# Emptying the merges' PSUM results by one engine each, and moving the output's scaled part, in a gated delta-rule block

## The chip, the cores and the metric

The kernel runs on one core of one Trainium2 chip. The metric is device time in microseconds of one execution. The kernel before was run three times: median 951.15 us, lowest 949.65, highest 952.15.

## The reference

One residual block with 512 tokens of width 1024, batch 1, all in float32. Two token mixers run on the normalised input: a gated delta rule with 8 heads of width 128, and a convolution branch with a causal depthwise convolution over 31 frames. Their gated sum goes through an output projection; a SwiGLU channel mixer with 2816 hidden units and a last RMSNorm follow. The part that matters here is the delta rule, cut to its core:

```python
kk = jnp.einsum("bnhid,bnhjd->bnhij", k, k)
m_low = jnp.where(strict, beta[..., :, None] * kk * decay, 0.0)
t_mat = m_low + jnp.eye(CHUNK)
sol = lax.linalg.triangular_solve(t_mat, rhs, left_side=True, lower=True, unit_diagonal=True)
u, w = sol[..., :DV], sol[..., DV:]
...
def step(S, xs_c):
    v_new = u_c - w_c @ S
    o_c = qd_c @ S + a_c @ v_new
    S = S * el_c + k_dec_c.T @ v_new
    return S, o_c
```

For each head a unit lower triangular system is solved per chunk, and a state S of 128x128 runs over the chunks.

## The kernel before, in words

**Stages.** The first stage makes all projections of the normalised input (query, key, value and output gate of each head, the two halves of the convolution branch, the branch gates) and, woven into them, the delta rule and the 31-tap convolutions. The attention output projection, the convolution branch's projection, the output projection and the channel mixer follow. The change lies in the first stage alone, from about 100 to 435 us of the span.

**Projections.** Float32 weights are split into a high and a low part: `unit` loads a 128x1024 piece, ScalarE rounds it (`whi`, L111) and VectorE subtracts (`wlo`, L112). A product is three matmuls with 512 columns each (`split3`, L121). `proj` yields after each of the eight row blocks, so one step of the driver is three such matmuls. There are three buffers for weight pieces, so ScalarE's next L111 often waits for TensorE to finish with an older piece.

**The order of the work.** The loop at the end of the stage (`while step() or chains`) takes one projection step at a time. `count` is the number of steps done. The delta rule of a head is a Python generator (`chain`); each `yield n` puts its next piece n steps later, so that a product of the chain stands n projection steps behind the operations that make its operands. The chain of head h begins 32 + `OTHERS[h]` steps after the one before. The framework turns the traced order into a fixed order on each engine when the kernel is built: by priority, which is the order of tracing, among what it thinks ready, with all waits added by it. `behind()` puts a piece of the chain behind the last marked projection operation of each engine. The 31-tap convolutions (`conv31`) are traced with a priority lowered by `OFF`, so they fill VectorE where it has nothing else ready: 30 operations of 512 columns a channel block (L690), accumulating in one PSUM bank. After the eighth block the sum over blocks (`sacc`, L696) is the operand of L709, the first product of the layer norm, which stands in TensorE's order among the products of the attention output projection.

**The chain of a head.** The kernel uses chunks of 128 tokens, four per head, and inverts the triangular matrices by doubling: GpSimd makes the inverses of 16-wide diagonal blocks (L499 to L504), and three merges make 32, 64 and 128-wide inverses. A merge is two products after one another, each for two pairs of chunks (`group`, L526), into one PSUM tile (`psb`, a pool with a single buffer, tile name `b`), and each result is emptied to SBUF, partly transposed in 32x32 blocks:

- The 16-wide merge ends in L574 and L575 on VectorE.
- The 32-wide merge's first product is emptied by L587. Its second is emptied by six operations, L595 to L600, in turn on ScalarE (copies) and VectorE (transposes). L595 and L596 write `m64`, the operand of the next merge; L597 to L600 write `Y`, the inverse that is being built. L601 copies one corner of `Y`.
- The 64-wide merge's first product is emptied by L605 (ScalarE) and L606 (VectorE), its second by L609 (ScalarE) and L610 (VectorE).

Then the recurrence runs over n = 0 to 3 with one PSUM tile a step (`pst`, a single buffer of one bank, tile name `st`, four column blocks of 128): L622 and L623 multiply the state by key and query (blocks 0 and 2), L625 on VectorE makes the right-hand side R, L628 applies `Y` to it (block 1), and L630 on ScalarE scales the result to the solution `w`. Three steps later L633 makes the state's update (block 0) and L634 the output's inner part (block 3). VectorE makes the new state (L640, or L638 for n = 0); ScalarE scales block 2 by the decay (`Ae`, L646), VectorE adds block 3 to it (L647; for n = 0, L643 copies block 3 alone) and ScalarE takes the sum of squares (L648). Three steps later the next n begins. L646 and L647 exist for n = 1, 2 and 3, 24 times in all.

The framework keeps the accesses of different engines to one PSUM tile apart, reads among them: L596 starts when L595 has ended, though they read other partitions.

Of the kernel before, what the change touches and what calls it, by code (L numbers as in the profile page):

```python
# [6 lines left out]
F32 = mybir.dt.float32  # L7
F32R = mybir.dt.float32r
I32 = mybir.dt.int32
AF = mybir.ActivationFunctionType  # L10
# [4 lines left out]
P = 128  # L15
# [17 lines left out]
def block_kernel(ctx, tc, a):  # L33
    nc = tc.nc
    V, S, G, PE = nc.vector, nc.scalar, nc.gpsimd, nc.tensor
# [176 lines left out]
    with tc.tile_pool(name="st", bufs=2) as st:  # L212
# [78 lines left out]
        ps = psg.tile([P, 4, P], F32, name="g")  # L291
# [61 lines left out]
        beta, nbeta, kdf, egc, negc, egl, nmc = (sm[:, i] for i in range(7))  # L353
# [28 lines left out]
    gp = ph1.enter_context(tc.tile_pool(name="gp", bufs=1))  # L382
    gps_.append(gp)
    Ys = [gp.tile([P, NT, P], F32, name="Y%d" % i) for i in range(2)]
    st16, st32, st64 = ([gp.tile([P, 2, P], F32, name="s%d%d" % (w, i)) for i in range(2)] for w in (16, 32, 64))
    m64 = gp.tile([P, 2, 64], F32, name="m64")
# [3 lines left out]
    def even_odd(t):  # L390
        return t.rearrange("p (q e) c -> p e q c", e=2)
# [137 lines left out]
    def chain(h, kT, qT, ss, kd, b2, Un, cp, Vp, at, yq, zs):  # L529
        sq, Y = junk[:, 0:P], Ys[h % 2]  # L530
        flat = lambda t: t.rearrange("p n c -> p (n c)")
        b32 = [slice(32 * b, 32 * b + 32) for b in range(4)]
        lo64, hi64 = slice(0, 64), slice(64, P)
        ev, od = slice(0, 2), slice(2, 4)
        Ue, Uo = (even_odd(Un)[:, e] for e in range(2))


        cT = gp.tile([P, 2, 32], F32, name="cT")
        V.transpose(out=flat(cT), in_=flat(cp[:, od]))
        s1 = gp.tile([P, 2, 32], F32, name="s1")  # L540
        S.activation(s1[:, :, 0:16], cT[:, :, 0:16], AF.Copy, scale=mh2)
        S.activation(s1[:, :, 16:32], cp[:, ev, 16:32], AF.Copy, scale=mh1)
        for b in b32:
            S.copy(out=st16[0][b, :, b], in_=s1[b])
        yield 3
        for i in (0, 2):
            S.copy(out=st32[0][b32[i], :, b32[i + 1]], in_=Ue[b32[i], :, b32[i + 1]])
            V.transpose(out=st32[0][b32[i + 1], :, b32[i]], in_=Uo[b32[i], :, b32[i + 1]])
        yield 3
        S.copy(out=st64[0][lo64, :, hi64], in_=Ue[lo64, :, hi64])  # L550
        S.copy(out=st64[0][hi64, :, lo64], in_=Uo[lo64, :, hi64])
        yield 3


        YY = gp.tile([P, NT, 32], F32, name="YY")
        XX = gp.tile([P, NT, 32], F32, name="XX")
        S.activation(YY[:, :, 0:16], yq, AF.Copy, scale=mh1)
        S.activation(YY[:, :, 16:32], yq, AF.Copy, scale=mh2)
        V.transpose(out=flat(XX), in_=flat(YY))
        Xe, Xo, Ye, Yo = XX[:, ev], XX[:, od], YY[:, ev], YY[:, od]  # L560
        m = gp.tile([P, 2, 16], F32, name="m16")
        V.tensor_tensor(out=m, in0=Xe[:, :, 0:16], in1=Yo[:, :, 16:32], op=ALU.add)
        s2 = gp.tile([P, 2, 32], F32, name="s2")
        S.copy(out=s2[:, :, 16:32], in_=Ye[:, :, 16:32])
        S.copy(out=s2[:, :, 0:16], in_=Xo[:, :, 0:16])
        for b in b32:
            S.copy(out=st16[1][b, :, b], in_=s2[b])
        yield 3
        ps = group(16, st16[0], m)
        Q = gp.tile([P, 2, 16], F32, name="Q16")  # L570
        S.activation(Q, ps, AF.Copy)
        yield 3
        ps = group(16, st16[1], Q)
        V.scalar_tensor_tensor(out=Xe[:, :, 0:16], in0=ps, scalar=mh2, in1=Xe[:, :, 0:16], op0=ALU.mult, op1=ALU.add)  # L574
        V.scalar_tensor_tensor(out=Yo[:, :, 16:32], in0=ps, scalar=mh1, in1=Yo[:, :, 16:32], op0=ALU.mult,  # L575
                               op1=ALU.add)
        m = gp.tile([P, 2, 32], F32, name="m32")
        for i, b in enumerate(b32):
            (S.copy if i < 2 else V.tensor_copy)(out=m[b], in_=Yo[b] if i % 2 else Xe[b])
        V.transpose(out=flat(Xo), in_=flat(Yo))  # L580
        V.transpose(out=flat(Ye), in_=flat(Xe))
        for i, b in enumerate(b32):
            S.copy(out=st32[1][b, :, b], in_=Ye[b] if i % 2 else Xo[b])  # L583
        yield 4
        ps = group(32, st32[0], m)
        Q = gp.tile([P, 2, 32], F32, name="Q32")
        S.activation(Q, ps, AF.Copy)  # L587
        for i in range(2):
            S.copy(out=m64[b32[i], :, b32[i]], in_=Xe[b32[i]])
            S.copy(out=m64[b32[i + 2], :, b32[i]], in_=Xo[b32[i]])  # L590
        for b in b32:
            S.copy(out=Y[b, :, b], in_=YY[b])  # L592
        yield 4
        ps = group(32, st32[1], Q)
        S.copy(out=m64[b32[1], :, b32[0]], in_=ps[b32[1]])  # L595
        V.transpose(out=m64[b32[3], :, b32[0]], in_=ps[b32[0]])  # L596
        S.copy(out=Y[b32[2], od, b32[3]], in_=ps[b32[2]])  # L597
        V.transpose(out=Y[b32[2], ev, b32[3]], in_=ps[b32[3]])
        S.copy(out=Y[b32[0], od, b32[1]], in_=ps[b32[0]])
        V.transpose(out=Y[b32[0], ev, b32[1]], in_=ps[b32[1]])  # L600
        S.copy(out=Y[lo64, ev, hi64], in_=Y[hi64, od, hi64])  # L601
        yield 5

        ps = group(64, st64[0], m64)
        S.activation(st64[1][hi64, :, hi64], ps[hi64], AF.Copy)  # L605
        V.tensor_copy(out=st64[1][lo64, :, lo64], in_=ps[lo64])  # L606
        yield 4
        ps = group(64, st64[1], Y[:, ev, hi64])
        S.activation(Y[lo64, ev, hi64], ps[hi64], AF.Copy)  # L609
        V.tensor_copy(out=Y[lo64, od, hi64], in_=ps[lo64])  # L610
        yield 3


        o = gp.tile([P, NT, P], F32, name="o", bufs=3)
        Sp = None
        for n in range(NT):

            ps = pst.tile([P, 4, P], F32, name="st")
            if n == 0:
                R = Vp[:, 0, :]  # L620
            else:
                PE.matmul(ps[:, 0, :], kT[:, n, :], Sp, start=True, stop=True)  # L622
                PE.matmul(ps[:, 2, :], qT[:, n, :], Sp, start=True, stop=True)  # L623
                R = gp.tile([P, P], F32, name="R", bufs=3)
                V.scalar_tensor_tensor(out=R, in0=ps[:, 0, :], scalar=negc[:, n, h:h + 1], in1=Vp[:, n, :],  # L625
                                       op0=ALU.mult, op1=ALU.add)
                yield 3
            PE.matmul(ps[:, 1, :], Y[:, n % 2 * 2 + n // 2, :], R, start=True, stop=True)  # L628
            w = gp.tile([P, P], F32, name="w", bufs=2)
            S.activation(w, ps[:, 1, :], AF.Copy, scale=b2[:, n:n + 1])  # L630
            yield 3
            if n < NT - 1:
                PE.matmul(ps[:, 0, :], kd[:, n, :], w, start=True, stop=True)  # L633
            PE.matmul(ps[:, 3, :], at[:, n, :], w, start=True, stop=True)  # L634
            if n < NT - 1:
                Sn = gp.tile([P, P], F32, name="S", bufs=2)
                if n == 0:
                    V.tensor_copy(out=Sn, in_=ps[:, 0, :])  # L638
                else:
                    V.scalar_tensor_tensor(out=Sn, in0=Sp, scalar=egl[:, n, h:h + 1], in1=ps[:, 0, :],  # L640
                                           op0=ALU.mult, op1=ALU.add)
            if n == 0:
                V.tensor_copy(out=o[:, 0, :], in_=ps[:, 3, :])  # L643
            else:
                Ae = gp.tile([P, P], F32, name="R", bufs=3)
                S.activation(Ae, ps[:, 2, :], AF.Copy, scale=egc[:, n, h:h + 1])  # L646
                V.tensor_tensor(out=o[:, n, :], in0=ps[:, 3, :], in1=Ae, op=ALU.add)  # L647
            S.activation(sq, o[:, n, :], AF.Square, accum_out=ss[:, 2, n:n + 1])  # L648
            if n < NT - 1:
                Sp = Sn  # L650
                yield 3

        V.tensor_scalar(out=ss[:, 3], in0=ss[:, 1], scalar1=EPS, scalar2=EPS * 128.0, op0=ALU.add, op1=ALU.mult)
        V.scalar_tensor_tensor(out=ss[:, 3], in0=ss[:, 2], scalar=1.0 / 128.0, in1=ss[:, 3],
                               op0=ALU.mult, op1=ALU.add)
        tc.keep_in_program_order(G.tensor_tensor(out=ss[:, 4], in0=ss[:, 3], in1=half4, op=ALU.pow))
        ended.append([count[0], False, (h, o, ss, zs)])
# [182 lines left out]
    while step() or chains:  # L840
# [4 lines left out]
        for c in list(chains):  # L845
            if c[0] <= count[0] or not queue:
                with behind():
                    n = next(c[1], None)
# [35 lines left out]
    for j in range(KD):  # L884
# [5 lines left out]
        ps = psm.tile([P, T], F32, name="mm")  # L890
# [11 lines left out]
    for j in range(KD):  # L902
        ps = psm.tile([P, T], F32, name="mm")
# [413 lines left out]
    for c, b in ((0, bank), (256, bank2)):  # L1317
        ps = b()[:, c:c + 256]
# [68 lines left out]
```

## Time and profile before

One execution was profiled. It took 953.04 us; its span, from the first to the last instruction, is 951.3 us.

| what | before |
|---|---|
| median of three runs | 951.15 us |
| profiled execution, its span | 953.04 us, 951.3 us |
| granted TensorE clock, mean | 0.997 |
| ScalarE (ACT) busy | 560.8 us, 1277 instructions |
| GpSimd (POOL) busy | 330.7 us, 541 instructions |
| moved by DMA | 177.39 MB |

In the profile PE is TensorE's matmuls and PEld its weight loads, DVE is VectorE, ACT ScalarE, POOL GpSimd and SP the engine that issues most DMAs. A float32 matmul that is not split appears as two instructions. Names such as `b<-m,s` read "output from inputs" without buffer numbers. The view of waits lists who waited for whom, in total, how many times, and the longest; when an engine waited for several things, the one that came last is named, and that is sometimes a bystander. The timeline lists start, length, engine, line and shape, with the idle time before the instruction in brackets. Ends of matmuls are modelled: they are pipelined, and drawn longer than the distance at which they follow one another.

### The profile page before, as it was taken

To read this page: it belongs to the slowest core of one execution; us is meant where nothing else is said; L and a number is where in the kernel's file an instruction comes from. 1 tells how busy PE (TensorE), PEld (TensorE's weight loads), DVE (VectorE), ACT (ScalarE), POOL (GpSimd) and SP (SyncE) were. 2 spreads that over 40 slices of the span, in tenths; PEclk is the share of its full clock that TensorE was granted. 3 is DMA by queue.
4 is the path that set the end of the run, shared out by engine and by line. 5 is a ranking of instruction groups with operands and counts; after the bars stand their busy time and mean duration, and the time that the engine had idled before them with its cause. 6 is when DMAs were issued, how large, how long until landed. Compare 5 with 4: busy or idle time off the path is not lost.

```text
span 951.3 us, 14518 instructions
## 1 busy us (share of the span) xinstructions
PE 928.8 (98%) x4952; PEld 785.9 (83%) x4952; DVE 740.5 (78%) x1157; ACT 560.8 (59%) x1277; POOL 330.7 (35%) x541
## 2 busy tenths in 40 slices
PE   9999999999999999999899999999999999999996
PEld 6778787878887888788778888888889999988885
DVE  4899598888888889899988643676636877888896
ACT  6698887878778786634447323333334454556545
POOL 0045524243443437544034350254441111133042
PEclk9999999999999999999999999999999999999999
DMA  9333322222222236998988983598898555567654
GB/s 321 110 134 104 122 90 78 99 92 68 84 90 87 99 135 148 312 280 268 283 274 253 274 255 131 174 290 285 279 251 233 174 188 187 178 220 253 226 182 150
DMA packets 78187, 177.39 MB, mean 186 GB/s; under 512 B 10080, under 2 KB 19472, under 8 KB 77088
## 3 DMA queue, kind: packets, MB, share of 16 engines
q1 hardware_dynamic: 66528, 144.89, 44.4%
q0 software_dynamic: 10288, 28.90, 13.1%
q10 hardware_dynamic: 1296, 2.67, 0.7%
q8 instruction: 39, 0.64, 0.3%
q14 instruction: 36, 0.29, 0.1%
HBM read 156.22 MB, written 45.37 MB: 212 GB/s over the span
## 4 chain that ended last, share of the span: by engine, by line
PE 70%; ACT 12%; DVE 6%; issue 3%; POOL 3%; DMA 1%; SPq 0%; POOLq 0%; ACTq 0%; DVEq 0%
PE mm L121 44%; PE w L121 20%; ACT whi L111 1%; DVE wlo L112 1%; PE b L526 1%; DVE cps L690 1%; DVE acc L422 1%; DMA sgd<-sg 1%; ACT Y L592 1%; ACT s L583 1%; ACT Un L473 1%; PE g L435 1%; ACT R L646 0%; PE st L628 0%; POOL y L504 0%
## 5 line engine op out<-in xcount | busy, mean ns | idle before, releaser
L111 ACT ACTIVATE whi<-raw 128x1024 fp32r<-128x1024 f32 (+1 forms) x191 | 196.6, 1030 | 250.5 <-PE mm L121 163.6
L112 DVE TENSOR_TENSOR wlo<-raw,whi 128x1024 fp32r<-128x1024 f32 (+1 forms) x191 | 238.0, 1246 | 82.0 <-ACT whi L111 80.2
L121 PE MATMUL mm<-hh,whi 128*128 128x512 f32 (+1 forms) x688 | 268.7, 391 | 0.3 <-ACT hh L336 0.3
L121 PE MATMUL mm<-hl,whi 128*128 128x512 f32 (+1 forms) x688 | 263.3, 383 | 0.0
L121 PE MATMUL mm<-hh,wlo 128*128 128x512 f32 (+1 forms) x688 | 263.1, 383 | 0.0
L690 DVE SCALAR_TENSOR_TENSOR cps<-c,c31w,cps 128x512 f32<-128x512 f32 x240 | 179.8, 749 | 4.2 <-ACT cps L688 0.5
L121 PEld LDWEIGHTS mm<-hh,wlo 128*128 128x128 f32 x688 | 129.6, 188 | 23.2
L121 PEld LDWEIGHTS mm<-hh,whi 128*128 128x128 f32 x688 | 129.9, 189 | 21.3 <-ACT hh L336 0.8
L121 PEld LDWEIGHTS mm<-hl,whi 128*128 128x128 f32 x688 | 130.0, 189 | 20.4
L1020 POOL TENSOR_TENSOR fm<-fm 128x256 f32<-128x256 f32 x33 | 30.6, 929 | 116.0 <-DVE s L1020 93.2
L422 DVE SCALAR_TENSOR_TENSOR acc<-mm,c4w,acc 128x511 f32<-128x511 f32 (+2 forms) x72 | 53.1, 741 | 3.2 <-ACT acc L419 3.0
L502 POOL TENSOR_TENSOR ytm<-U,y 128x60 f32<-128x60 f32 (+14 forms) x120 | 35.3, 294 | 50.2 <-DMA U<-sc 41.4
L196 POOL DMA_DIRECT2D s<-in_wgu_dram x24 | 22.9, 970 | 82.5 <-DMA s<-in_wgu_dram 82.5
L121 PE MATMUL mm<-yh,whi 128*128 128x512 f32 x128 | 51.2, 400 | 0.0
L121 PE MATMUL mm<-yl,whi 128*128 128x512 f32 x128 | 50.0, 391 | 0.0
L121 PE MATMUL mm<-yh,wlo 128*128 128x512 f32 x128 | 49.9, 390 | 0.0
L121 PE MATMUL w<-hh,wlo 128*128 128x256 f32 x168 | 47.7, 284 | 0.4 <-DVE wlo L112 0.4
L121 PE MATMUL w<-hh,whi 128*128 128x256 f32 x168 | 47.6, 284 | 0.0
L121 PE MATMUL w<-hl,whi 128*128 128x256 f32 x168 | 47.5, 283 | 0.0
L121 PE MATMUL w<-wlo,fh 128*128 128x512 f32 (+1 forms) x115 | 44.3, 385 | 0.2 <-DVE wlo L112 0.2
L121 PE MATMUL w<-whi,fl 128*128 128x512 f32 (+1 forms) x115 | 44.2, 385 | 0.0
L121 PE MATMUL w<-whi,fh 128*128 128x512 f32 (+1 forms) x115 | 44.2, 384 | 0.0
(344 smaller groups left out, 1927.9 us busy)
## 6 DMA issues: line engine op xcount, KB each, us to landing
raw<-in_win_dram SPq DMA_DIRECT2D x61, 512.0 KB, 3.3
raw<-in_wgu_dram SPq DMA_DIRECT2D x32, 512.0 KB, 3.4
s<-in_wgu_dram SPq DMA_DIRECT2D x48, 256.0 KB, 5.4
raw<-s SPq DMA_DIRECT2D x48, 256.0 KB, 3.7
raw<-wsum SPq DMA_DIRECT2D x44, 256.0 KB, 3.6
raw<-in_wdn_dram SPq DMA_DIRECT2D x33, 256.0 KB, 3.2
s<-in_wgu_dram POOLq DMA_DIRECT2D x24, 256.0 KB, 6.7
s<-s POOLq DMA_DIRECT2D x24, 256.0 KB, 6.8
```

The source lines that it names most:

```text
L111: marked(S.activation(hi, raw, AF.Copy), "unit")
L112: marked(V.tensor_tensor(out=lo, in0=raw, in1=hi.bitcast(F32), op=ALU.subtract), "unit")
L121: marked(PE.matmul(ps, l, r, start=first and i == 0, stop=last and i == 2))
L196: fed.append(nc.gpsimd.dma_start(*begun.pop(0), accum_op=ALU.add, max_dma_last_dim=2048))
L422: marked(V.scalar_tensor_tensor(out=acc[:, s:], in0=ps[:, :T - s], scalar=c4w[:, j, k:k + 1], in1=acc[:, s:], op0=ALU.mult, op1=ALU.add))
L435: PE.transpose(ps[:, n, :], src[:, n, :], ident)
L473: S.activation(Un[:, n, :], ps[:, n, :], AF.Copy, scale=nb2[:, n:n + 1])
L502: G.tensor_tensor(out=tm[:, :, 0:w], in0=U[:, k, :, k + 1:], in1=y[:, :, k:k + 1].broadcast_to([P, NT, w]), op=ALU.mult)
L526: PE.matmul(ps[:, q, 0:w], stationary[:, q, :], moving[:, q, :], start=True, stop=True)
L583: S.copy(out=st32[1][b, :, b], in_=Ye[b] if i % 2 else Xo[b])
L690: V.scalar_tensor_tensor(out=acc, in0=c[:, k:k + T], scalar=c31w[:, i, k:k + 1], in1=acc, op0=ALU.mult, op1=ALU.add)
L1020: return eng.tensor_tensor(out=out, in0=in0, in1=in1, op=op)
```

## The change

The second product of the 32-wide merge is copied whole to a new SBUF tile `Z` by one ScalarE operation, and the six operations that read PSUM read `Z`. Of the 64-wide merge, the first product is emptied by ScalarE alone (L606 moves to it) and the second by VectorE alone (L609 moves to it). In the recurrence the scaling of block 2 (`Ae`) is traced right behind `w` in place of behind the new state.

```diff
         ps = group(32, st32[1], Q)
-        S.copy(out=m64[b32[1], :, b32[0]], in_=ps[b32[1]])
-        V.transpose(out=m64[b32[3], :, b32[0]], in_=ps[b32[0]])
-        S.copy(out=Y[b32[2], od, b32[3]], in_=ps[b32[2]])
-        V.transpose(out=Y[b32[2], ev, b32[3]], in_=ps[b32[3]])
-        S.copy(out=Y[b32[0], od, b32[1]], in_=ps[b32[0]])
-        V.transpose(out=Y[b32[0], ev, b32[1]], in_=ps[b32[1]])
+        Z = gp.tile([P, 2, 32], F32, name="Z")
+        S.activation(Z, ps, AF.Copy)
+        S.copy(out=m64[b32[1], :, b32[0]], in_=Z[b32[1]])
+        V.transpose(out=m64[b32[3], :, b32[0]], in_=Z[b32[0]])
+        S.copy(out=Y[b32[2], od, b32[3]], in_=Z[b32[2]])
+        V.transpose(out=Y[b32[2], ev, b32[3]], in_=Z[b32[3]])
+        S.copy(out=Y[b32[0], od, b32[1]], in_=Z[b32[0]])
+        V.transpose(out=Y[b32[0], ev, b32[1]], in_=Z[b32[1]])
...
         ps = group(64, st64[0], m64)
         S.activation(st64[1][hi64, :, hi64], ps[hi64], AF.Copy)
-        V.tensor_copy(out=st64[1][lo64, :, lo64], in_=ps[lo64])
+        S.activation(st64[1][lo64, :, lo64], ps[lo64], AF.Copy)
         yield 4
         ps = group(64, st64[1], Y[:, ev, hi64])
-        S.activation(Y[lo64, ev, hi64], ps[hi64], AF.Copy)
+        V.tensor_copy(out=Y[lo64, ev, hi64], in_=ps[hi64])
         V.tensor_copy(out=Y[lo64, od, hi64], in_=ps[lo64])
...
             S.activation(w, ps[:, 1, :], AF.Copy, scale=b2[:, n:n + 1])
+            if n:
+                Ae = gp.tile([P, P], F32, name="R", bufs=3)
+                S.activation(Ae, ps[:, 2, :], AF.Copy, scale=egc[:, n, h:h + 1])
             yield 3
...
-                Ae = gp.tile([P, P], F32, name="R", bufs=3)
-                S.activation(Ae, ps[:, 2, :], AF.Copy, scale=egc[:, n, h:h + 1])
                 V.tensor_tensor(out=o[:, n, :], in0=ps[:, 3, :], in1=Ae, op=ALU.add)
```

## The prediction

> **What bounds the kernel now.** I read the page first, then the table of waits, then the timeline around one merge and one recurrence step, and last the stretch in which the delta-rule stage hands over to the output projection. The page says where the time is:
>
> ```profile
> PE 928.8 (98%) x4952; PEld 785.9 (83%) x4952; DVE 740.5 (78%) x1157; ACT 560.8 (59%) x1277; POOL 330.7 (35%) x541
> ```
>
> TensorE is all but full, so the change can only give back time in which TensorE stands in front of a product that is not ready. The table of waits lists these stalls; its columns are microseconds in total, times, and the longest. The edited lines are behind three of them:
>
> ```profile
> PE b L526 <- DVE Y L600: 3.0, 5, 1.0
> ...
> PE mm L709 <- DVE sacc L696: 2.8, 1, 2.8
> ...
> PE st L622 <- DVE o L647: 1.3, 4, 0.4
> ...
> PE b L526 <- POOL y L504: 1.2, 1, 1.2
> ...
> PE st L622 <- DVE c L678: 0.8, 1, 0.8
> ```
>
> These figures understate the loss. The timeline of the last head's 32-wide merge shows why (start, length, engine, line):
>
> ```profile
> 396.71 0.20 ACT L595 COPY m<-b 32x64 f32<-32x64 f32 x1
> ...
> 396.94 0.24 DVE L596 STREAM_TRANSPOSE m<-b 32x64 f32<-32x64 f32 x1 [0.57 <-ACT m L595]
> ...
> 397.56 0.20 ACT L597 COPY Y<-b 32x64 f32<-32x64 f32 x1
> ...
> 398.36 0.25 DVE L598 STREAM_TRANSPOSE Y<-b 32x64 f32<-32x64 f32 x1
> ...
> 398.96 0.39 PE L121 MATMUL mm<-hl,whi 128*128 128x512 f32 x1
> ...
> 399.19 0.40 PE L121 MATMUL mm<-hh,wlo 128*128 128x512 f32 x1
> ...
> 399.43 0.24 DVE L600 STREAM_TRANSPOSE Y<-b 32x64 f32<-32x64 f32 x1
> ...
> 399.82 0.63 PE L526 MATMUL b<-m,s 128*128 128x64 f32 x4 [0.23 <-DVE Y L600]
> ```
>
> Projection products start 0.23 us apart (398.96, 399.19) although each is drawn 0.39 long. The merge's product starts 0.63 after the one before it: 0.40 lost, of which the view calls 0.23 idle. So each wait in the table costs 0.17 more than it says. The rows also show the mechanism. The six readers of the 32-wide product alternate between ScalarE and VectorE, each starts only after the one before it, and each hand-over queues behind other work, so emptying takes from 396.71 to 399.67. The next product needs that one PSUM bank, although its data (`m64`) was complete at 397.18.
>
> The first head has the same stall. The table books it on GpSimd because a GpSimd operation ended near it; L600 ends at 115.89, right before the product:
>
> ```profile
> 115.65 0.24 DVE L600 STREAM_TRANSPOSE Y<-b 32x64 f32<-32x64 f32 x1
> ...
> 116.04 0.29 PE L526 MATMUL b<-m,s 128*128 128x64 f32 x1 [1.21 <-POOL y L504]
> ```
>
> **The change part by part.** *Emptying the 32-wide merge through Z.* Removed: six waits of TensorE, 3.0 + 1.2 + 6 × 0.17 = 5.2 us. Added: one ScalarE copy of 128x64 from PSUM per head, and six operations now read SBUF. Prices of the nearest rows (mean ns of one is the number behind the comma):
>
> ```profile
> L587 ACT ACTIVATE Q<-b 128x64 f32<-128x64 f32 x8 | 1.7, 216 | 0.1
> ...
> L583 ACT COPY s<-YY 32x64 f32<-32x64 f32 x16 | 3.9, 243 | 0.6 <-DVE YY L581 0.2
> ...
> L595 ACT COPY m<-b 32x64 f32<-32x64 f32 x8 | 1.6, 204 | 0.2
> ```
>
> ```profile
> L548 DVE STREAM_TRANSPOSE s<-Un 32x64 f32<-32x64 f32 x16 | 3.8, 236 | 0.4
> ...
> L596 DVE STREAM_TRANSPOSE m<-b 32x64 f32<-32x64 f32 x8 | 1.9, 243 | 6.6 <-ACT m L595 6.3
> ```
>
> Z costs 0.22, eight times, so 1.7 us of ScalarE; the copies from SBUF cost 39 ns more each, 24 of them, so 0.9 us. ScalarE is 59% busy, and this lies in its slack. The merge's product will need Z (which frees the bank) and the two parts of `m64`. Z can start where L595 started, so both are ready near 397.2 to 397.4 in the rows above, with the product due at 399.42. I take the new wait as nothing; if VectorE reaches the first transpose two 0.75 us convolution taps late, it still holds. The price of losing that cover is at most the 5.2 won.
>
> [...]
>
> *The output's scaled part moves.* Before, it stands between two VectorE operations:
>
> ```profile
> 389.93 0.31 DVE L640 SCALAR_TENSOR_TENSOR S<-S,sm,st 128x128 f32<-128x128 f32 x1
> ...
> 390.16 0.75 DVE L690 SCALAR_TENSOR_TENSOR cps<-c,c31w,cps 128x512 f32<-128x512 f32 x1
> ...
> 390.56 0.37 ACT L646 ACTIVATE R<-st,sm 128x128 f32<-128x128 f32 x1
> ...
> 390.97 0.29 DVE L647 TENSOR_TENSOR o<-st,R 128x128 f32<-128x128 f32 x1
> ...
> 391.31 0.30 PEld L622 LDWEIGHTS st<-S,kT 128*128 128x128 f32 x2 [0.42 <-DVE o L647]
> ```
>
> L640, L646 and L647 read one bank in turn, and the next step's L622 starts 0.05 after the last of them. With L646 gone from there, L647 can follow L640 at once and end near 390.5, before the product is due. Removed: the four waits on L647, 1.3 + 4 × 0.17 = 2.0. A fifth, booked on L678 (0.8 + 0.17), is the same bank in the third head; I take half, 0.5, between 0 and 1.0.
>
> Added: L646 now reads the bank *before* L633 and L634 write other columns of it. L622 above writes the first quarter of the bank and yet waits for L647, which reads the last, so the wait goes by bank. [...] If only columns mattered, this addition would cost nothing. L633 and L634 are often tight already:
>
> ```profile
> PEld st L633 <- ACT w L630: 3.8, 10, 0.8
> ...
> PEld st L634 <- ACT w L630: 1.7, 3, 0.8
> ```
>
> ```profile
> 137.45 0.38 ACT L630 ACTIVATE w<-st,ss 128x128 f32<-128x128 f32 x1
> ...
> 137.70 0.34 ACT L541 ACTIVATE s<-cT,cst 128x32 f32<-128x32 f32 x1
> ...
> 137.88 0.49 PE L633 MATMUL st<-w,kd 128*128 128x128 f32 x2
> ```
>
> ```profile
> 345.15 0.49 PE L633 MATMUL st<-w,kd 128*128 128x128 f32 x2 [0.41 <-ACT w L630]
> ```
>
> The operation behind `w` starts 0.25 to 0.28 after it; of 0.37, it ends 0.27 after `w` does. Of the 24 steps with a scaled part, 10 have their product within 0.07 us of `w`'s end (these are the first and the last), and two more within 0.13 and 0.23: 10 × 0.27 + 0.3 = 3.0 us lost. Bounds: 0, if the ten were late for reasons that go, and 24 × 0.37 = 8.9.
>
> *Swapped engines.* L606 goes to ScalarE, right behind L605; its reader comes four steps later, so nothing. L609 goes to VectorE, so the first recurrence product waits for VectorE's queue in place of ScalarE's:
>
> ```profile
> DVE o L647 <- ACT R L646: 8.1, 9, 1.6
> ACT Y L609 <- PE b L526: 7.9, 4, 3.6
> ...
> PEld st L628 <- ACT Y L609: 1.2, 4, 0.4
> ```
>
> In four heads that product hangs on L609 already. Each can become late by up to one tap, 4 × 0.75 = 3.0, or by nothing; I take a quarter, 0.7, since the second copy's slot on VectorE was already close behind the first. Queued behind a waiting L609 are convolution taps and weight splits.
>
> Sum for TensorE: 5.2 + 2.0 + 0.5 − 3.0 − 0.7 = **4.0 us** won.
>
> **Does it reach the end?** Only if VectorE keeps up, because the next hand-over waits for its last tap:
>
> ```profile
> 471.94 1.06 ACT L111 ACTIVATE whi<-raw 128x1024 fp32r<-128x1024 f32 x1 [3.80 <-PE mm L121]
> ...
> 473.03 1.23 DVE L112 TENSOR_TENSOR wlo<-raw,whi 128x1024 fp32r<-128x1024 f32 x1 [0.17 <-ACT whi L111]
> 474.17 0.69 DVE L696 TENSOR_TENSOR sacc<-sacc,cv 128x512 f32<-128x512 f32 x1
> ...
> 474.91 1.22 PE L709 MATMUL mm<-sacc,cst 128*128 128x512 f32 x1 [2.79 <-DVE sacc L696]
> ```
>
> ```profile
> 434.00:475.00 41.00, 38.22 (x171) 31.29 (x170) 39.13 (x50) 18.13 (x28) 10.36 (x13) 0.99 0.89 275
> ```
>
> VectorE is 39.13 of 41 us busy here (third pair) and had 0.17 us to spare at 473.03. If it were no earlier, TensorE's gain would end as a longer wait at L709. But VectorE loses its own waits on L646, 8.1 us in nine, twice what it needs. So both come earlier by about 4. Behind L709 nothing of the change remains.
>
> The profiled execution took 953.04 us for a span of 951.3, and the sum makes it 949.0. It lies 1.9 above the median of the three runs, 951.15; carried over to that, **947.1 us**. A difference under 0.3% (2.9 us) cannot be told from none.
>
> **The rivals.** *VectorE does not follow.* The order on each engine is made at build time, and the taps may be dealt out differently. For it: 95% busy before L709. Against: the 8.1 us. Then the gain is 0.2 (the slack at 473.03) to 2 us, 949 to 951, no change. *The product waits for something else at once.* Z frees the bank, but the transposes into `m64` come late in VectorE's queue, by the 2.2 us between 397.18 and 399.42 or more. Then 5.2 is not won, and 4.0 − 5.2 = −1.2 gives 952.3, no change. *The scaled part does not get ScalarE's next slot.* Where a weight split of 1.06 us stands between `w` and it, the ten tight products are late by 0.27 + 1.06: 13.3 + 0.3 + 0.7 − 7.7 = 6.6 us slower, 957.8. It decides from a mean of (7.7 − 0.7 + 2.9) / 24 = 0.41 us added per step. For it: in most tight steps another ready operation came right behind `w`, as L541 did. Against: in program order the scaled part is now the next one of its chain.
>
> **How the numbers follow.** Forecast and anything else over 2.9 us: 0.55. VectorE not following 0.23 and the product waiting anew 0.09, both within 0.3%: 0.32. The last rival, slower: 0.13. The range reaches down to the sum without the added wait on the bank or on VectorE (7.7, so 943.4) and a little of the L709 stall, 943.0, and up to 952.4, past the second rival.
>
> **What would show it.** Right: no waits of L526 on L600 and of L622 on L647; L633 and L634 waiting on L646 at about a dozen steps, near 0.3 each; VectorE's waits on L646 gone; L709 some 4 us earlier with its wait still near 3. Wrong: L709's wait longer by what the merges won; L526 waiting on the transpose into `m64`; a weight split between L630 and the scaled part.

## The result, and the profile after

The changed kernel took 947.57 us (median of six runs, 944.63 to 948.72), the kernel before 951.65 (median of six, 949.65 to 952.92). The ratio of the times is 0.9955, with a 95% interval of 0.9936 to 0.9974: 4.1 us faster, where 4.0 had been forecast. The two profiled executions are further apart than the medians, 953.04 and 946.16 us. 1.1 us of that lies before the stage that was edited: the 300th projection matmul (counted from 0) starts at 89.4 in one trace and 88.3 in the other. Another 1.4 us is the granted clock at the hand-over (51.2 and 49.8 us in the table of all traces): 0.50 from 474.4 to 477.8 us in the first trace, 1.00 there in the second. Of the six runs of the changed kernel, the two with a mean granted clock of 0.998 and 0.999 (the profiled one among them) took 946.16 and 944.63 us, and the four at 0.995 and 0.996 took 947.47 to 948.72.

The page of the changed kernel (same columns as before) shows a shorter span, 944.4, and a little less busy time on every engine but GpSimd:

```profile
PE 925.9 (98%) x4952; PEld 783.8 (83%) x4952; DVE 736.9 (78%) x1157; ACT 559.9 (59%) x1285; POOL 333.2 (35%) x541
```

Lines have moved by a few: the scaled part is now L635, `w` L632, the two products behind it L638 and L639, the state times key L624, the sum of state and output L645 and L650, ScalarE's copies of the 64-wide merge L607 and L608, VectorE's L611 and L612, the convolution tap L693, the sum over blocks L699 and the layer norm's first product L712. This is the view of TensorE's waits from 95 to 475 us:

```profile
PE mm L712 <- DVE sacc L699: 2.8, 1, 2.8
PE st L638 <- ACT R L635: 0.9, 3, 0.4
...
PE st L639 <- ACT R L635: 0.5, 1, 0.5
...
PE b L526 <- ACT s L608: 0.2, 1, 0.2
```

The waits of L526 on L600 and of the state's product on L647 (now L624 on L650) are gone from it. In their place the two products wait for the scaled part, as forecast, and one of the merge's products waits for a copy that the change put on ScalarE. The weight loads' view shows the same waits where TensorE still had a matmul running:

```profile
PEld st L638 <- ACT R L635: 3.5, 7, 0.8
...
PEld st L639 <- ACT R L635: 2.2, 5, 0.9
...
PEld b L526 <- ACT s L608: 0.7, 2, 0.4
```

The last head's 32-wide merge in the timeline:

```profile
390.48 0.22 ACT L596 ACTIVATE Z<-b 128x64 f32<-128x64 f32 x1
...
390.74 0.24 DVE L598 STREAM_TRANSPOSE m<-Z 32x64 f32<-32x64 f32 x1 [1.08 <-ACT Z L596]
...
391.00 0.24 DVE L600 STREAM_TRANSPOSE Y<-Z 32x64 f32<-32x64 f32 x1
...
391.21 0.24 ACT L597 COPY m<-Z 32x64 f32<-32x64 f32 x1
...
391.26 0.23 DVE L602 STREAM_TRANSPOSE Y<-Z 32x64 f32<-32x64 f32 x1
...
393.33 0.55 PE L526 MATMUL b<-m,s 128*128 128x64 f32 x4
```

The bank is free at 390.70, 0.22 us after emptying began, where it took 2.96 before. The two engines no longer alternate, and the product at 393.33 follows the projections at the usual distance. One step of the recurrence in the same stretch:

```profile
383.99 0.31 DVE L645 SCALAR_TENSOR_TENSOR S<-S,sm,st 128x128 f32<-128x128 f32 x1
...
384.22 0.28 DVE L650 TENSOR_TENSOR o<-st,R 128x128 f32<-128x128 f32 x1
...
385.31 0.38 PE L624 MATMUL st<-S,kT 128*128 128x128 f32 x2
```

The output's sum now follows the new state at once, and the next product, 0.8 us after it, does not wait. The hand-over to the layer norm:

```profile
466.45 1.22 DVE L112 TENSOR_TENSOR wlo<-raw,whi 128x1024 fp32r<-128x1024 f32 x1 [0.17 <-ACT whi L111]
467.60 0.68 DVE L699 TENSOR_TENSOR sacc<-sacc,cv 128x512 f32<-128x512 f32 x1
468.33 0.30 PEld L712 LDWEIGHTS mm<-sacc,cst 128*128 128x128 f32 x2 [3.21 <-DVE sacc L699]
468.33 1.12 PE L712 MATMUL mm<-sacc,cst 128*128 128x512 f32 x2 [2.78 <-DVE sacc L699]
```

It comes 6.6 us earlier than before (474.91), 1.1 of which lies ahead of the stage, with the same wait and the same 0.17 to spare on VectorE.

### The profile page after: what moved, and what is told of

The parts are those of the page before. It is cut to its first block, busy times and chain, and to the rows that moved or that the text cites. A ratio compares the mean times of both kernels' runs of the same rounds, so it can differ in the third digit from the quotient of the medians.

```text
span 944.4 us, 14557 instructions
## 1 busy us (share of the span) xinstructions
PE 925.9 (98%) x4952; PEld 783.8 (83%) x4952; DVE 736.9 (78%) x1157; ACT 559.9 (59%) x1285; POOL 333.2 (35%) x541
## 4 chain that ended last, share of the span: by engine, by line
PE 77%; ACT 9%; DVE 3%; issue 2%; DMA 2%; POOL 1%; POOLq 0%; ACTq 0%; DVEq 0%; SPq 0%
PE mm L121 52%; PE w L121 19%; PE b L526 2%; ACT whi L111 1%; DMA raw<-s 1%; DVE wlo L112 1%; PE st L639 1%; PE g L435 1%; PE g L470 1%; ACT s L544 1%; ACT Vp L512 1%; PE st L630 1%; ACT Un L473 1%; POOL DT L444 1%; ACT pa L520 1%
## 5 line engine op out<-in xcount | busy, mean ns | idle before, releaser
L121 PE MATMUL mm<-hh,whi 128*128 128x512 f32 (+1 forms) x688 | 269.1, 392 | 0.3 <-ACT hh L336 0.3
L121 PE MATMUL mm<-hh,wlo 128*128 128x512 f32 (+1 forms) x688 | 263.0, 383 | 0.0
L121 PE MATMUL mm<-hl,whi 128*128 128x512 f32 (+1 forms) x688 | 262.5, 382 | 0.0
L693 DVE SCALAR_TENSOR_TENSOR cps<-c,c31w,cps 128x512 f32<-128x512 f32 x240 | 179.8, 749 | 5.6 <-ACT cps L691 1.7
L121 PEld LDWEIGHTS mm<-hh,wlo 128*128 128x128 f32 x688 | 129.6, 188 | 23.6
L121 PEld LDWEIGHTS mm<-hh,whi 128*128 128x128 f32 x688 | 129.8, 189 | 21.2 <-ACT hh L336 0.8
L121 PEld LDWEIGHTS mm<-hl,whi 128*128 128x128 f32 x688 | 130.0, 189 | 20.5
L502 POOL TENSOR_TENSOR ytm<-U,y 128x60 f32<-128x60 f32 (+14 forms) x120 | 36.6, 305 | 49.8 <-DMA U<-sc 41.0
L121 PE MATMUL mm<-yh,whi 128*128 128x512 f32 x128 | 50.6, 395 | 0.0
L121 PE MATMUL mm<-yh,wlo 128*128 128x512 f32 x128 | 49.8, 389 | 0.0
L121 PE MATMUL mm<-yl,whi 128*128 128x512 f32 x128 | 49.8, 389 | 0.0
L121 PE MATMUL w<-hh,wlo 128*128 128x256 f32 x168 | 47.8, 284 | 0.3 <-DVE wlo L112 0.3
L121 PE MATMUL w<-hh,whi 128*128 128x256 f32 x168 | 47.6, 284 | 0.0
L121 PE MATMUL w<-hl,whi 128*128 128x256 f32 x168 | 47.5, 283 | 0.0
L121 PE MATMUL w<-wlo,fh 128*128 128x512 f32 (+1 forms) x115 | 44.4, 386 | 0.1
L121 PE MATMUL w<-whi,fl 128*128 128x512 f32 (+1 forms) x115 | 44.2, 385 | 0.0
L121 PE MATMUL w<-whi,fh 128*128 128x512 f32 (+1 forms) x115 | 44.2, 385 | 0.0
```

The lines of the kernel that those rows point to most:

```text
L121: marked(PE.matmul(ps, l, r, start=first and i == 0, stop=last and i == 2))
L502: G.tensor_tensor(out=tm[:, :, 0:w], in0=U[:, k, :, k + 1:], in1=y[:, :, k:k + 1].broadcast_to([P, NT, w]), op=ALU.mult)
L693: V.scalar_tensor_tensor(out=acc, in0=c[:, k:k + T], scalar=c31w[:, i, k:k + 1], in1=acc, op0=ALU.mult, op1=ALU.add)
```

## The experiments

Three theories stood against each other. A: the gain is the stalls of TensorE that the edits remove. B: it comes from the moved scaled part alone, through VectorE. C: every build draws a new order of the engines, and this moves the time whatever the edit is for. The first four kernels ran on one chip, beside a median of 951.62 for the kernel before.

### Z alone

Edit: the first part of the change, `Z` and its six readers, in the kernel before.

> Z alone: the 32-wide merge is emptied through Z, the other two parts are as before. Theory A (the gain is the bank of the 32-wide merge coming free sooner): the waits of L526 on the last transpose go, 5.2 us in the sum, and the time falls by 4 to 5 us, ratio about 0.995. Theory B (the gain comes from the scaled part, which lets VectorE follow at once and frees the recurrence's bank): time within 1 us of before. Theory C (any new order of the engines moves the time by some microseconds, and the edits matter little): anything from -4 to +4 us, with no link to the stalls of TensorE.

Measured: 947.65 us, ratio 0.9962 (0.9949 to 0.9976): 4.0 us faster, as theory A has it, and nearly all of the change's gain. Theory C's range, 4 us either way, holds it too.

### The scaled part alone

```diff
             S.activation(w, ps[:, 1, :], AF.Copy, scale=b2[:, n:n + 1])
+            if n:
+                Ae = gp.tile([P, P], F32, name="R", bufs=3)
+                S.activation(Ae, ps[:, 2, :], AF.Copy, scale=egc[:, n, h:h + 1])
             yield 3
```

(and its old place removed).

> The scaled part alone is moved behind w. Theory A with the terms of the prediction: waits on the recurrence's bank of 2.5 us go, 3.0 us come at L633 and L634, so within 1 us of before. Theory A as the changed kernel's trace has it (stalls in front of L622 3.6 us fewer, in front of L633 and L634 only 0.4 more): 3 us faster, ratio about 0.997. Theory B: 4 us or more faster.

Measured: 968.19 us, ratio 1.0176 (1.0162 to 1.0190), 16.6 us slower. Neither A nor B allows for that. TensorE's waits in this kernel (L710 is the layer norm's first product):

```profile
PE mm L710 <- DVE sacc L697: 16.5, 1, 16.5
PE mm L121 <- ACT whi L111: 5.0, 1, 5.0
PE st L636 <- ACT R L633: 1.4, 3, 0.6
```

The 16.5 us stand in one place, far from the edit, and the waits on the moved operation are small.

### The swap alone

```diff
-        V.tensor_copy(out=st64[1][lo64, :, lo64], in_=ps[lo64])
+        S.activation(st64[1][lo64, :, lo64], ps[lo64], AF.Copy)
...
-        S.activation(Y[lo64, ev, hi64], ps[hi64], AF.Copy)
+        V.tensor_copy(out=Y[lo64, ev, hi64], in_=ps[hi64])
```

> The 64-wide merge alone is emptied by one engine per product. By the prediction's terms 0.7 us slower. By the changed kernel's trace, in which four of the merge's last products wait 1.4 us in all for ScalarE's second copy, 1 to 1.5 us slower, ratio about 1.001. Theory B: within 0.5 us.

Measured: 951.14 us, ratio 0.9994 (0.9984 to 1.0004). No difference: the two expectations of a loss missed, and theory B's, within 0.5 us, held.

### The scaled part twice

In the changed kernel:

```diff
             if n:
+                Ae = gp.tile([P, P], F32, name="R2", bufs=2)
+                S.activation(Ae, ps[:, 2, :], AF.Copy, scale=egc[:, n, h:h + 1])
                 Ae = gp.tile([P, P], F32, name="R", bufs=3)
```

> The changed kernel with the scaled part made twice, the first copy unused: 24 more reads of the recurrence's bank by ScalarE, 0.28 us apart, ahead of L633 and L634. If a read there costs what the prediction took (0.27 at ten or more of the 24 steps), about 3 us slower than the changed kernel, that is some 1 us faster than before. If the products mostly have room (0.4 us for the first read, as the trace of the changed kernel has it), 0.5 to 1.5 us slower than the changed kernel.

Measured: 958.27 us, ratio 1.0072 (1.0059 to 1.0085) to before, so 10.7 us slower than the changed kernel. Both expectations, 3 us and 0.5 to 1.5 us, missed. The trace again has the loss in one place:

```profile
PE mm L714 <- DVE sacc L701: 11.3, 1, 11.3
```

### Where the late sum comes from

The eight convolution blocks share one PSUM bank. Each begins and ends with a ScalarE operation of lowered priority (L688 and L692 in the kernel before). In the trace of the slow kernel with the scaled part alone, 95 ScalarE instructions and 32 us lie between the end of the second block and the start of the third; in the kernel before there is none. In the kernel with the scaled part twice the gap stands between the third block and the fourth, 40 instructions and 13 us. (The expectations below count rows of the order as built, 66 and 64; the traces of those two runs have 94 and 95 instructions there.) So theory C became one mechanism, D: a block that misses its place on ScalarE leaves VectorE without taps, and the sum that ends the stage comes late. The order of a kernel can be read before it runs, so D could be made to predict. Two kernels were chosen whose builds have such a gap, and two in which it cannot arise. They ran beside 950.86 for the kernel before.

### Two lines exchanged

```diff
-        S.copy(out=Y[b32[2], od, b32[3]], in_=ps[b32[2]])
-        V.transpose(out=Y[b32[2], ev, b32[3]], in_=ps[b32[3]])
         S.copy(out=Y[b32[0], od, b32[1]], in_=ps[b32[0]])
         V.transpose(out=Y[b32[0], ev, b32[1]], in_=ps[b32[1]])
+        S.copy(out=Y[b32[2], od, b32[3]], in_=ps[b32[2]])
+        V.transpose(out=Y[b32[2], ev, b32[3]], in_=ps[b32[3]])
```

> The kernel before with two lines exchanged with the two behind them in the emptying of the 32-wide merge; the work and its dependences stay. If edits count through the stalls of TensorE that they name, within 1 us of before. If the order on the engines decides (Theory D: a convolution block that misses its place on ScalarE leaves VectorE without taps, and the layer norm's sum comes late): in this build 66 rows of ScalarE stand between the end of the second block and the start of the third, 0 to 6 in the kernel before, so 8 to 17 us slower, with the added time in front of the layer norm's first product.

Measured: 968.43 us, ratio 1.0186 (1.0172 to 1.0200). The same work in a different order of lines costs 17.6 us, a little more than the 8 to 17 expected. ScalarE's timeline from 165 to 202 us shows the gap, first in the kernel before, where block three starts 0.6 us after the emptying of block two does:

```profile
167.39 0.59 ACT L692 ACTIVATE cv<-cps 128x512 f32<-128x512 f32 x1
168.01 0.78 ACT L688 ACTIVATE cps<-c,vec,c31w 128x512 f32<-128x512 f32 x1
```

and then with the lines exchanged, where it starts 34.5 us later:

```profile
164.56 0.60 ACT L692 ACTIVATE cv<-cps 128x512 f32<-128x512 f32 x1
...
199.10 0.77 ACT L688 ACTIVATE cps<-c,vec,c31w 128x512 f32<-128x512 f32 x1
```

VectorE's taps (L690) in the stretch from 95 to 200 us, busy time and count, before and with the lines exchanged:

```profile
95.00:200.00 105.00, 36.13 (x49) 1.00 0.26 89
```

```profile
95.00:200.00 105.00, 23.08 (x32) 0.98 0.29 87
```

Seventeen taps, 13 us of VectorE's time, are put off, and 15 of them start only after 475 us, where the kernel before has none left. TensorE waits for them:

```profile
PE mm L709 <- DVE sacc L696: 15.3, 1, 15.3
PE mm L121 <- ACT whi L111: 4.7, 1, 4.7
```

### Z and the scaled part, without the swap

> The changed kernel without the swap of engines at the 64-wide merge. By the stalls of TensorE: 0.7 to 1.5 us faster than the changed kernel, some 5 us faster than before. By Theory D: this build has 64 rows of ScalarE between the second block's end and the third's start, so 8 to 15 us slower than the changed kernel and slower than before, with the added time in front of the layer norm's first product.

Measured: 967.84 us, ratio 1.0170 (1.0154 to 1.0186). The swap, which did nothing by itself, stands between this and the changed kernel's 947.57; the wait in front of the layer norm is 15.3 us again. Theory D's forecast from the order held in sign and place. The loss against the changed kernel, 20.3 us, was above the 8 to 15 expected; 4.9 of it is a wait of a projection for its weight piece, of the kind in the second row above:

```profile
PE mm L712 <- DVE sacc L699: 15.3, 1, 15.3
PE mm L121 <- ACT whi L111: 4.9, 1, 4.9
```

### The same edits with the blocks' ends and starts at ordinary priority

```diff
     def conv31(i, c):
         acc = psc.tile([P, T], F32, name="cps")
+        prio = tc.cur_priority
+        tc.cur_priority = prio - OFF
         S.activation(acc, c[:, 0:T], AF.Identity, scale=c31w[:, i, 0:1], bias=dw_b[:, i:i + 1])
+        tc.cur_priority = prio
...
+        prio = tc.cur_priority
+        tc.cur_priority = prio - OFF
         S.activation(cv[i], acc, AF.Copy)
+        tc.cur_priority = prio
```

First with the scaled part alone, which had been the slow kernel:

> The scaled part alone is moved, as in the run that was 16.6 us slower, and the first and last ScalarE operation of each convolution block get the priority of ordinary work in place of the lowered one. Theory D: the 15 us in front of the layer norm's first product go, and the kernel is 0 to 3 us faster than before. If the read of the bank ahead of the two products is itself what costs: still more than 8 us slower than before.

Measured: 945.05 us, ratio 0.9935 (0.9923 to 0.9948). The 16.6 us are gone and more with them: it is 5.8 us faster than before, where 0 to 3 had been expected. The wait at the layer norm is no longer in the table. Then with the whole change:

> The changed kernel with the same raised priority of the blocks' ends and starts. Theory D: no worse than the changed kernel, which had no large miss; VectorE has its taps earlier, so the wait in front of the layer norm's first product (2.8 us) may shrink: 0 to 4 us faster than the changed kernel. If that wait is set by the weight piece ahead of the sum on VectorE: no difference.

Measured: 942.66 us, ratio 0.9913 (0.9899 to 0.9928). This beats both kernels; by the ratios it is 4.0 us faster than the changed kernel, the upper end of theory D's range. The layer norm's first product (L718 here) stands in the timeline without a wait:

```profile
465.99 1.02 PE L718 MATMUL mm<-sacc,cst 128*128 128x512 f32 x2
```

### How much of it is the change

Four more kernels with the same raised priority, beside 951.17 for the kernel before, were to tell what the edits bring when the sum is never late. They ran on another chip than the runs above, so a comparison with those goes by the ratios to the kernel before. The kernel before with nothing else edited:

> The kernel before with the raised priority of the convolution blocks' ends and starts alone, none of the change. The layer norm's first product waited 2.8 us in the view of waits (3.7 against the usual distance); that goes, so 3 to 4 us faster than before. The merge's stalls on L600 (5.2 us) and on L647 (2.0) stay. If raised priority alone explained the fastest run, it would be 8 us faster.

Measured: 945.68 us, ratio 0.9940 (0.9927 to 0.9953): 5.5 us faster, more than the wait alone; the stage is shorter too (343.4 for 345.8 us in the table below), and at the hand-over (46.7 for 51.2) the clock no longer falls to 0.50. With Z:

> Raised priority, and Z alone of the change. Theory A: 4 to 5 us faster than raised priority alone, as Z alone was against before (4.0).

Measured: 945.63 us, ratio 0.9941 (0.9927 to 0.9955). Z brings nothing here. Theory A misses. TensorE's waits from 88 to 500 us, first without and then with Z:

```profile
PE b L526 <- DVE Y L600: 1.7, 2, 1.1
PE st L622 <- DVE o L647: 1.1, 2, 0.7
...
PE st L634 <- ACT w L630: 0.8, 1, 0.8
```

```profile
PE st L624 <- DVE o L649: 1.3, 2, 0.9
PE st L636 <- ACT w L632: 1.2, 2, 0.7
PE st L635 <- ACT w L632: 1.1, 2, 0.7
```

The merge's wait on its last transpose is gone, and the products behind `w` wait more: by the distances between starts, the stalls of the first fall by 3.2 us and those of the second grow by 2.3. With Z and the scaled part:

> Raised priority, Z and the moved scaled part, without the swap of engines at the 64-wide merge. This pair (without raised priority 17 us slower than before) should be within 1.5 us of raised priority with the whole change; if the swap costs what the first trace suggested, 0.7 to 1.5 us faster than that.

Measured: 950.79 us, ratio 0.9999 (0.9990 to 1.0007), 0.0086 in the ratio or some 8 us slower than with the swap, so the expectation of 1.5 us at most missed. The sum is in time, but a single projection waits for its weight piece, which stands on ScalarE behind some twenty short operations of the chain:

```profile
242.24 0.79 PE L121 MATMUL mm<-hh,whi 128*128 128x512 f32 x1 [4.65 <-ACT whi L111]
```

The slow builds above have this wait too (5.0 and 4.7 in their tables). It is a second accident of the order, and raising the blocks' priority does not prevent it. Last, the whole change with the scaled part twice:

> Raised priority and the whole change with the scaled part made twice. Against the same with the scaled part once: 3 us slower if a read ahead of L633 and L634 costs 0.27 at ten steps or more, as predicted; 0.5 to 1.5 us slower if most of these products have room. The 10 us by which doubling slowed the changed kernel itself should not return, if they were the late sum.

Measured: 947.13 us, ratio 0.9956 (0.9943 to 0.9969), 0.0043 in the ratio or some 4 us slower than with it once. Its trace holds a wait of the same kind:

```profile
PE mm L121 <- ACT whi L111: 3.3, 2, 3.1
PE st L640 <- ACT R L637: 1.6, 3, 0.6
PE st L641 <- ACT R L637: 0.8, 2, 0.6
```

The 10 us did not return. The 4 us are mostly that wait. In front of the two products the stalls grow from 4.5 to 5.8 us, so 1.3, of the size of the second expectation; in the changed kernel doubling left them as they were (4.6 and 4.4).

All traces together, worked out from the starts of the L121 matmuls: the stage is the time from the 300th to the 1400th, the hand-over from the 1400th to the 1600th (us, counted from 0). From the 1600th to the 2700th every kernel takes 235.4.

```
                                   stage  hand-over  median
before                             345.8    51.2     951.15
the change                         340.3    49.8     947.57
Z alone                            342.1    49.7     947.65
swap alone                         344.7    52.7     951.14
scaled part alone                  347.8    65.2     968.19
lines exchanged                    349.5    64.6     968.43
Z and scaled part                  349.9    64.4     967.84
the change, scaled part twice      343.4    59.9     958.27
with the blocks' priority raised:
before                             343.4    46.7     945.68
Z alone                            344.0    46.7     945.63
scaled part alone                  344.1    46.7     945.05
Z and scaled part                  349.3    46.7     950.79
the change                         341.0    46.7     942.66
the change, scaled part twice      346.0    46.7     947.13
```

The hand-over column holds one thing more than the wait for the sum. Where TensorE waits there, in all traces but two, its granted clock falls from 1.00 to 0.50 for a stretch that begins after the wait has begun and ends after it: from 474.4 to 477.8 us in the trace before, whose wait lasts from 472.1 to 474.9, for 6.8 us with the swap alone, and for 17.1 us with the lines exchanged, where the projections behind the wait start 0.43 us apart in place of 0.23. In the two, the change and Z alone, the wait is the same 2.8 us, and the clock stays at 1.00. So the 1.4 us between the hand-overs of the kernel before and the change are the clock of these two executions; the wait did not get shorter.

## Why the prediction was right, and which terms were not

The forecast of 947.1 met 947.57, and the signs that it named were there. The mechanism was right for this pair: the stalls that it named went, and no longer wait at the hand-over took their place. Its terms, in stalls of TensorE beyond the usual distance between starts, in this pair of traces (good to some 0.3 us, since the usual distance has to be chosen):

- *The 32-wide merge, 5.2 us won.* Stalls in front of these products fell from 5.6 to 0.2. Right in this pair of orders, and Z alone measured 4.0; with the raised priority Z alone brought nothing.
- *The recurrence's bank, 2.0 + 0.5 won.* In front of L622 they fell from 4.2 to 0.6: 3.6, a little more.
- *The scaled part ahead of L633 and L634, 3.0 lost.* This term was mis-sized: 4.4 before, 4.6 after, so 0.2. The step that failed priced the later read at the distances of the old trace and took the products' place among the projections as fixed. The build moves it. Between L628 and the product behind `w` stand 296 projection matmuls in all 32 steps before, and 339 after (for the first head's last step 4 and then 9). With 0.23 us each, the products stand some 10 us later in sum, and projections fill the time. Ten to twelve products still wait, but for the scaled part in place of `w`, and for as long as before. In the four pairs of kernels that differ in the scaled part alone, these stalls change by -0.1 (before and the scaled part alone), 0.9 (with Z), 0.6 and 0.0 us (the same with the raised priority), so that the term is small is shown. The reason is not: with the scaled part alone only 4 more projections stand there than before (300), and the stalls are just as few.
- *L606 to ScalarE, nothing; L609 to VectorE, 0.7 lost.* The other way round: stalls in front of L628 went from 1.2 to 1.0, while the merge's last products, some of which wait for the second copy on ScalarE, lost 1.4. That the swap causes this is not shown: it is 0.4 in the trace of the swap alone and 1.4 in that of Z and the scaled part without the swap.
- *VectorE follows.* It did: the hand-over came 6.6 us earlier, 5.5 of it from the stage, and its wait stayed at 2.8, as the prediction said.

These terms add up to 7.6 us (5.4 + 3.6 - 0.2 + 0.2 - 1.4), 3.6 more than the forecast's 4.0, most of it from the scaled part. Other short products of the chain lost 1.3, which the prediction did not count, and the stage as a whole is 5.5 us shorter in this pair. So the error at the scaled part was offset by losses that the prediction did not count, and because this pair of executions lies further apart than the medians. That the median meets the forecast within 0.5 us is therefore partly luck. The order that the build drew was luck too: two exchanged lines alone moved the kernel before by 17.6 us. That the first rival, VectorE not following, could only cost the gain was wrong by more: in four kernels it cost 9 to 14 us at the hand-over, because the taps do not merely fail to come earlier, they are dealt out later. The prediction saw that the taps might be dealt out differently, but did not look at what starts a block of them.

What is shown: the stalls that the edits name shrink with the edit. In front of the 64-wide merge's first product they are 2.6 to 5.6 us in the six kernels without Z and 0.2 to 2.1 in the eight with it; in front of the state's product (L622) 2.9 to 5.2 in the six without the moved scaled part and 0.3 to 1.4 in the eight with it. And the loss at the hand-over follows the place of the blocks' starts in ScalarE's order. What stays open is how much of the 4.1 us belongs to the edits. With the hand-over held at 46.7, the whole change brings 2.6 us by the ratios (0.9940 and 0.9913, whose intervals just touch), Z alone nothing and the scaled part 0.5 at most, within the noise; without the raised priority Z alone brings 4.0. The removed stalls come back in part as others, differently in each order, and six orders do not average this out.

## What to carry to other kernels

Where the framework fixes the order of the engines at build time, compare an edit of a microsecond or two with a build in which only the order differs; here two exchanged lines weighed four times as much as the change. Before trusting such a comparison, look for what stands at low priority on a busy engine and starts a long run of work on another, and give that start its own place. A PSUM result with several readers on two engines is worth trying with one copy when its bank is what the next product waits for: here the stalls in front of that product went from 5.6 to 0.2 us, while the copy alone (Z) brought 4.0 us of time in one order of the engines and nothing in the other.

## What the runs showed of the hardware that was not expected

A ScalarE copy of 128x64 out of PSUM took 0.22 us and, in the last head, replaced a hand-over of 2.96 us. Transposes of 32x64 on VectorE took 0.23 to 0.24 us from SBUF and 0.24 to 0.25 from PSUM, so moving all 24 of them to SBUF gave VectorE itself 0.2 us.

Between 88 and 500 us of the 14 traces, the granted clock of TensorE fell from 1.00 to 0.50 at each of its waits of 3.1 us or more (up to 16.5 us in the view of waits), at two of the four waits of 2.8 us, and nowhere else. The falls began 1 to 5 us after the last product ahead of the wait and lasted 3.4 to 17.1 us. Such a wait cost more than its own length: at the layer norm's first product the clock stayed at 0.50 for 2.9 us after the wait of 2.8 in the kernel before, and for 4.9 us after that of 15.3 with the lines exchanged.
